# Two layers of a hybrid encoder on one core: activation tiles 2080 bytes apart, modulation blocks dealt out anew, a tenth convolution block on TensorE

## The chip, the core and the metric

The kernel runs on one core of a Trainium2 chip: TensorE (matmul), VectorE, ScalarE, GpSimd and SyncE, each with a queue of its own that it works through in order, and DMA queues between the chip's main memory and SBUF, the on-chip memory of 128 partitions. SyncE issues nearly all loads of weights. The metric is the device time of one execution, in microseconds. The time given is the median of several runs; beside it stands one profiled execution with its trace.

## The reference

An input of 256 tokens by 2048 features passes two layers, all in 32-bit floats. Each layer has a token mixer and a gated convolution feed-forward, and each of these four sub-layers f does

```
x <- x + gate * RMSNorm_post(f(RMSNorm_pre(x) * (1 + scale) + shift))
```

where shift, scale and gate (six vectors of 2048 a layer) are products of silu(c), a conditioning vector, with a matrix ada_w of 2048 by 12288 per layer. Layer 0's mixer is a convolution module: h @ w_in (2048 to 4096), a gated product, a causal depthwise convolution of width 31, a layer norm with SiLU, and @ w_out (2048 to 2048). Layer 1's mixer is gated linear attention with four heads: projections q, k, v, r and a gate, chunks of 64 tokens, @ w_out. The feed-forward is

```
a, b = split(h @ w_in)            # 2048 -> 2 * 5632
y = (silu(causal_dwconv(a, 3 taps)) * b) @ w_out
```

## The kernel before

All weights stream once through SBUF in blocks of 128 by 2048 floats, 1 MB each. The list `items` (from line 242) holds every block in the order of use. `Stream` loads them, four blocks ahead (eight during the convolution mixer), from SyncE: `load` takes a buffer from the pool `raw`, or from a second pool `cols` of four buffers for the modulation blocks that belong to layer 0's mixer and to shift and scale of its feed-forward. `_process` splits a weight block in two halves of 1024 columns: `hi`, a rounded copy made by ScalarE (line 120), and `lo`, the rest, made by VectorE (line 124). Matrix products are then sums of products of hi and lo parts. The pool `parts` holds four halves of hi and four of lo, so the split is at most one or so blocks ahead of TensorE.

The modulation vectors come from blocks of ada_w that are dealt among the weight blocks with `fill` (rows) and `fillc` (columns). A *row* block holds 128 outputs, and VectorE multiplies it with silu(c), laid out in all partitions, and sums along it, in one instruction (line 361, `ada_row`). A *column* block goes through TensorE (line 376, `ada_col`), whose result is transposed by VectorE and summed by small matmuls (line 392). A row or column block's work is done when the stream passes it (`flush`).

Two forms of product matter. `mm_block` has a weight block stationary and an activation tile moving: a matmul of 512 columns for hi (256 tokens, high and low part of the activation side by side, line 438) and one of 256 columns for lo (line 440), in runs of eight each. It serves fa and fb, the two halves of the feed-forward's first product, and q, k, r of the attention. `mm_tokens` has the activation stationary and 512 columns of weights moving (lines 609 to 611, three matmuls for a contraction tile and a token half): `ps_fo`, the second feed-forward product, `ps_cout` and `ps_gout`, the mixers' output products, and `ps_v`. The activation tiles are 128 by 512 floats, 2048 bytes in a partition, sixteen of them: the normed tiles h (and uc, the convolution's result) in `hpool`, the feed-forward's u and the attention's o in `upool`. A few weight blocks are split into hpool tiles (`st.spare`, line 974 and others), so that the last column group has all its weights at hand.

The convolution mixer (line 685) first runs the steps of h @ w_in (`ps_cin`). Then a loop (line 880) interleaves, per turn: one early column block, seven steps of the convolution on TensorE (`taps_pe`), eight taps on VectorE (`taps_dve`, line 801, 30 for a block of 128 channels), and the sums for the layer norm (`statistics`). Of sixteen channel blocks nine (`PE_BLOCKS`) go over TensorE: 16 matmuls that lay out shifted copies (`ps_late`, line 829), 32 with tap matrices `zt` built by VectorE (line 839) or ScalarE (line 843), into `ps_conv` (line 845). Seven go over VectorE. After the loop, four more column blocks fill TensorE while VectorE finishes the layer norm, and then the output product runs column group by column group. `ROWS_COUT` and `COLS_COUT` say how many modulation blocks lie behind each of its sixteen weight blocks; 16 rows (shift of the feed-forward) and 4 columns lie there.

In the feed-forward (line 944) 44 pairs of fa and fb run in groups of 16, 16 and 12; behind each group come its ps_fo blocks, four column groups of four (or three) blocks. A row block lies behind each pair from the fourth on, and behind each ps_fo block but the last three. When a gate's sixteen rows are in, GpSimd writes the gate to main memory and reads it back into all partitions (`gate_rows`, line 589).

Of the kernel before, what the change touches and what calls it, by code (L numbers as in the profile page):

```python
# [7 lines left out]
F32 = mybir.dt.float32  # L8
F32R = mybir.dt.float32r
BF16 = mybir.dt.bfloat16  # L10
AF = mybir.ActivationFunctionType
ALU = mybir.AluOpType

P = 128
D = 2048
# [9 lines left out]

RUN = 8

PE_BLOCKS = (5, 7, 9, 10, 11, 12, 13, 14, 15)

NA = 12  # L30

STEPS = ((0, 2, 0, 16), (2, 2, 0, 16), (4, 4, 0, 16), (8, 4, 0, 8), (12, 4, 0, 8), (8, 8, 8, 16))

ADA = ((2, 1, 1, 0), (3, 3, 2, 0), (1, 1, 1, 1, 1, 1, 1, 1), (3, 3, 2, 0), (1,) * 4, (1,) * 8)
COLS_CONV = 12

GLA_ORDER = [
    (w[:-1], int(w[-1]))
# [6 lines left out]
    ).split()  # L45
]
COLS_COUT = (0, 0, 0, 0), (0, 1, 0, 1), (0, 1, 0, 1), (0, 0, 0, 0)
ROWS_COUT = (0, 0, 0, 4), (2, 1, 2, 1), (2, 1, 2, 1), (0, 0, 0, 0)
GROUPS = ((0, 16), (16, 16), (32, 12))


# [12 lines left out]
class Stream:  # L64
# [3 lines left out]
    def __init__(self, tc, ctx, items, ada_row, ada_col, raw_bufs=4, split_bufs=4):  # L68
        self.tc = tc
        self.nc = tc.nc  # L70
        self.items = items
        self.ada_row = ada_row
        self.ada_col = ada_col
        self.raw = ctx.enter_context(tc.tile_pool(name="raw", bufs=raw_bufs))
        self.parts = ctx.enter_context(tc.tile_pool(name="parts", bufs=split_bufs))
        self.cols = None
        self.ahead = raw_bufs
        self.loaded = 0
        self.done = 0
        self.pos = 0  # L80
        self.raws = {}
        self.tiles = {}
        self.late = []

        self.spare = {}
        self.sums = []
        self.hold = None
        self.first = SPLIT_FIRST
        self.index = {it["key"]: i for i, it in enumerate(items)}
# [87 lines left out]
        return (lambda a, w=P: part(his, a, w)), (lambda a, w=P: part(los, a, w))  # L177


class Later(list):  # L180


# [9 lines left out]
def trunk_kernel(ctx: ExitStack, tc: tile.TileContext, x, cvec, ccol, adar, adac, adah, par, taps, wgate,  # L192
                 cin, cout, gin, gv, gout, fin, fout, out):
    nc = tc.nc
    V, A, G = nc.vector, nc.scalar, nc.gpsimd
    PS = bass.MemoryType.PSUM

    const = ctx.enter_context(tc.tile_pool(name="const", bufs=1))
    hpool = ctx.enter_context(tc.tile_pool(name="hpool", bufs=16))
    ypool = ctx.enter_context(tc.tile_pool(name="ypool", bufs=8))  # L200
    dram = ctx.enter_context(tc.tile_pool(name="dram", bufs=2, space=bass.MemoryType.DRAM))
    small = ctx.enter_context(tc.tile_pool(name="small", bufs=2))
# [5 lines left out]

    pr = const.tile([P, NPAR], F32, tag="pr", name="pr")
    A.dma_start(out=pr[:, :C_DWB], in_=par[:, :C_DWB])  # L210
    ones = const.tile([P, P], F32, tag="ones", name="ones")
    G.memset(ones, 1.0)
    zeros = const.tile([P, 1], F32R, tag="zeros", name="zeros")
    G.memset(zeros.bitcast(F32), 0.0)
    epsb = const.tile([P, 1], F32, tag="epsb", name="epsb")
    G.memset(epsb, EPS)
    onec = const.tile([P, 1], F32, tag="onec", name="onec")
    G.memset(onec, 1.0)
    table = const.tile([P, 1], F32, tag="table", name="table")
    A.activation(table, onec, AF.Silu)  # L220

# [22 lines left out]
    def item(kind, key, src, n=D):  # L244
        early = key[0] == "col" or key[:2] == ("row", 0) and key[2] != 5
        items.append(dict(kind=kind, key=key, src=src, n=n, early=early))

    def wblk(key, src, n=2048):
        item("w", key, src, n)

    rows, cols = [], []

    def fill(n):
        for l, m, k in rows[:n]:
            item("row", ("row", l, m, k), adar[l, m * KT + k])
        del rows[:n]

    def fillc(n):
        for l, m, k, nk, i in cols[:n]:
            item("col", ("col", l, m, k, nk, i), adac[m, k // 4, i] if nk == 4 else adah[1 - m, k // 2, i])  # L260
        del cols[:n]
# [31 lines left out]
                else:  # L293
                    fillc(1)
    assert not ada
    early_cols = list(cols[: COLS_CONV + 4])
    fillc(COLS_CONV + 4)
    for c in range(4):
        for i in range(4):
            wblk(("cout", c, i), cout[i, c])  # L300
            n = COLS_COUT[c][i]
            fillc(n)
            fill(ROWS_COUT[c][i])
    assert not cols
    assert not rows

    def ffn_items(l):
        for g, (p0, np_) in enumerate(GROUPS):
            for j in range(p0, p0 + np_):
                wblk(("fa", l, j), fin[l, j])  # L310
                wblk(("fb", l, j), fin[l, NF + j])
                fill(j > 2)
            for c in range(4):
                for i in range(np_ // 4):
                    wblk(("fo", l, g, c, i), fout[l, p0 // 4 + i, c])
                    fill(g < len(GROUPS) - 1 or c < 3)

    rows += [(0, 5, k) for k in range(KT)]
    rows += [(1, m, k) for k in range(KT) for m in (1, 0)]
# [79 lines left out]
    apool = {}  # L399
# [12 lines left out]
    pp = {"ps": ctx.enter_context(tc.tile_pool(name="psum", bufs=6, space=PS))}  # L412
# [45 lines left out]
        return A.activation(junk, src, AF.Square, accum_out=ss[t][:, c : c + 1])  # L458

    def new_sums(name):  # L460
        return [small.tile([P, 4], F32, tag=f"ss{t}", name=f"ss{name}{t}") for t in range(2)]

    def most(ss, name):

        b = small.tile([P, 1], F32, tag="tb", name="tb" + name)
        V.tensor_reduce(b, ss[:, :3], mybir.AxisListType.X, ALU.add)
        V.tensor_scalar(b, b, 1.0 / D, EPS, ALU.mult, ALU.add)
        return b

    def token_rstd(ss, b, name):  # L470
        r = small.tile([P, 1], F32, tag="tr", name="tr" + name)
        apool["root"] = A.activation(r, ss[:, 3:], AF.Sqrt, bias=b, scale=1.0 / D)
        V.reciprocal(r, r)
        return r

    def warm(func, src):

        d = small.tile([P, 1], F32, tag="warm", name="warm")
        A.activation(d, src[:, :1], func, scale=0.0, bias=onec)

    def rstd_of(acc, n, name):
# [17 lines left out]
    def token_diag(ss, name):  # L499

        r = token_rstd(ss, most(ss, name), name)
        dg = small.tile([P, P], F32, tag="dgx", name="dgx" + name, bufs=2)
        apool["dg"] = V.tensor_scalar_mul(dg, ident, r)
        return dg
# [180 lines left out]
    def conv_mixer(l):  # L685
        with early as cx:
# [4 lines left out]
            ss = new_sums("in")  # L691
# [82 lines left out]
            def gather(j, ps, last):  # L774
# [7 lines left out]
                if last:  # L782
# [4 lines left out]
                    V.tensor_mul(zp, zp, g)  # L787
                    if j in PE_BLOCKS:
                        on_pe.append((j, zp))
# [87 lines left out]
            apool["sums"] = lambda name: pp["ps"].tile([P, 2 * T], F32, tag="ps", name=name)  # L877
            gap = early_cols[COLS_CONV:]
            del early_cols[COLS_CONV:]
            while len(squared) < KT:  # L880
# [7 lines left out]
            assert not early_cols  # L888
            zs = [zs[j] for j in range(KT)]
            warm(AF.Sqrt, mean_a)  # L890
            r = small.tile([P, T], F32, tag="rstd", name="r_ln", bufs=1)
            line = []
# [15 lines left out]
            with tc.high_priority(SPLIT_FIRST):  # L908
# [7 lines left out]
                root = A.activation(r, r, AF.Sqrt, bias=epsb)  # L916
# [21 lines left out]
                st.spare["cout", 3, i] = st.cols, "raw", D  # L938
            dg = proj_out("cout", us, l, 1, 2, room)
            st.ahead = 4  # L940
        pp["u"] = ctx.enter_context(tc.tile_pool(name="upool", bufs=16))
        return dg

    def ffn(l, dg, last):
# [265 lines left out]
def program():  # L1210
    import concourse.bacc as _bacc

    nc = _bacc.Bacc("TRN2", target_bir_lowering=False, num_devices=1)
    args = [nc.dram_tensor(f"in_{n}", s, F32, kind="ExternalInput").ap() for n, s in _DRAM]
    args.append(nc.dram_tensor("out_0_dram", (2, P, D), F32, kind="ExternalOutput").ap())
    with tile.TileContext(nc) as tc:
        trunk_kernel(tc, *args)
    return nc


def layout(inp):
# [21 lines left out]
    late = late.transpose(1, 4, 2, 3, 0).reshape(P, KT, 32)  # L1243
    taps[:, PE_BLOCKS] = late[:, PE_BLOCKS]
    fw = g["ffn_conv_w"].reshape(2, FW, NF, P).transpose(3, 0, 2, 1).reshape(P, 2 * NF * FW)
# [30 lines left out]
```

## Time and profile before

| | |
|---|---|
| median of 3 runs | 2356.03 us (2354.91 to 2356.15) |
| profiled execution, its own time | 2360.2 us |
| its span, first to last instruction | 2358.5 us |
| mean granted clock of TensorE | 0.988 |
| TensorE busy | 2301.0 us (98%) |
| VectorE busy | 1767.7 us (75%) |
| ScalarE busy | 1208.9 us (51%) |
| read from main memory | 604.69 MB, 257 GB/s over the span |

The span is from the first to the last instruction of the profiled execution; its time holds 1.7 us around that. A matmul's duration in the trace is longer than the distance to the next one, as matmuls are pipelined: the distance of two starts is its cost in a dense run. Rows of the trace that are quoted below give start, duration (or busy time), engine, line, operation, output and inputs by the program's names, the shapes, a count (x8) and, in brackets, how long the engine had been idle and what ended that.

### The profile page before, as it was taken

To read this page: it belongs to the slowest core of one execution; us is meant where nothing else is said; L and a number is where in the kernel's file an instruction comes from. 1 tells how busy PE (TensorE), PEld (TensorE's weight loads), DVE (VectorE), ACT (ScalarE), POOL (GpSimd) and SP (SyncE) were. 2 spreads that over 40 slices of the span, in tenths; PEclk is the share of its full clock that TensorE was granted. 3 is DMA by queue.
4 is the path that set the end of the run, shared out by engine and by line. 5 is a ranking of instruction groups with operands and counts; after the bars stand their busy time and mean duration, and the time that the engine had idled before them with its cause. 6 is when DMAs were issued, how large, how long until landed. Compare 5 with 4: busy or idle time off the path is not lost.

```text
span 2358.5 us, 34325 instructions
## 1 busy us (share of the span) xinstructions
PE 2301.0 (98%) x13616; PEld 1935.1 (82%) x13616; DVE 1767.7 (75%) x2550; ACT 1208.9 (51%) x1884; POOL 16.8 (1%) x44
## 2 busy tenths in 40 slices
PE   7999998899999999999999999999999999999998
PEld 5888756688878888888888888888888888888886
DVE  3889979688878888878977877756887466655665
ACT  5334354565534554345565576656554455534553
POOL 0000000000000000000000000000000000000000
PEclk8999999899999999999999999999999999999999
DMA  9988767667799878988947756463778555555553
GB/s 385 368 325 342 286 198 300 253 236 293 288 301 355 296 286 320 362 280 314 362 161 265 277 211 229 165 229 130 294 273 282 196 188 190 196 182 195 194 202 120
DMA packets 86722, 609.05 MB, mean 258 GB/s; under 512 B 10081, under 2 KB 10401, under 8 KB 13601
## 3 DMA queue, kind: packets, MB, share of 16 engines
q1 hardware_dynamic: 84944, 602.47, 69.4%
q0 software_dynamic: 1472, 4.23, 0.7%
q8 instruction: 106, 1.74, 0.3%
q14 instruction: 56, 0.45, 0.1%
q10 hardware_dynamic: 144, 0.16, 0.0%
HBM read 604.69 MB, written 2.13 MB: 257 GB/s over the span
## 4 chain that ended last, share of the span: by engine, by line
PE 91%; DVE 4%; DMA 3%; issue 1%; ACT 1%; SPq 0%; another core or an unknown queue 0%; DVEq 0%; ACTq 0%
PE ps_fb L438 14%; PE ps_fa L438 13%; PE ps_fa L440 7%; PE ps_fb L440 7%; PE ps_fo L610 7%; PE ps_fo L611 7%; PE ps_fo L609 7%; PE ps_r L438 3%; PE ps_cin L870 2%; PE ps_cin L872 2%; PE ps_cin L871 2%; DMA raw<-in_adar 2%; PE ada L376 1%; DVE pair L801 1%; PE ps_k L438 1%; PE ps_r L440 1%
## 5 line engine op out<-in xcount | busy, mean ns | idle before, releaser
L124 DVE TENSOR_TENSOR lo<-raw,hi 128x1024 fp32r<-128x1024 f32 (+1 forms) x763 | 914.4, 1210 | 383.1 <-ACT hi L120 380.3
L120 ACT CAST hi<-raw 128x1024 fp32r<-128x1024 f32 (+1 forms) x760 | 786.1, 1044 | 809.6 <-PE ps_fa L438 183.6
L438 PE MATMUL ps_fa<-h,hi 128*128 128x512 f32 x1376 | 348.7, 395 | 0.0
L438 PE MATMUL ps_fb<-h,hi 128*128 128x512 f32 x1376 | 348.1, 395 | 0.0
L361 DVE CUSTOM_DVE_ANT_0 raw<-raw,cb 128x2048 f32<-128x2048 f32 x140 | 319.8, 2285 | 33.7 <-DMA raw<-in_adar 33.3
L438 PEld LDWEIGHTS ps_fa<-h,hi 128*128 128x128 f32 x1376 | 246.1, 188 | 46.1
L438 PEld LDWEIGHTS ps_fb<-h,hi 128*128 128x128 f32 x1376 | 245.8, 188 | 45.8
L610 PE MATMUL ps_fo<-lo,u 128*128 128x512 f32 x704 | 274.9, 390 | 5.0 <-DVE lo L124 5.0
L611 PE MATMUL ps_fo<-hi,u 128*128 128x512 f32 x704 | 274.7, 390 | 0.0
L609 PE MATMUL ps_fo<-hi,u 128*128 128x512 f32 x704 | 273.8, 390 | 0.0
L440 PEld LDWEIGHTS ps_fa<-h,lo 128*128 128x128 f32 x1376 | 182.5, 188 | 16.0 <-DVE lo L124 0.5
L440 PEld LDWEIGHTS ps_fb<-h,lo 128*128 128x128 f32 x1376 | 182.5, 188 | 15.6
L440 PE MATMUL ps_fa<-h,lo 128*128 128x256 f32 x1376 | 185.0, 277 | 0.0
L440 PE MATMUL ps_fb<-h,lo 128*128 128x256 f32 x1376 | 184.8, 277 | 0.0
L610 PEld LDWEIGHTS ps_fo<-lo,u 128*128 128x128 f32 x704 | 132.6, 188 | 32.9 <-DVE lo L124 5.4
L611 PEld LDWEIGHTS ps_fo<-hi,u 128*128 128x128 f32 x704 | 132.6, 188 | 27.7
L609 PEld LDWEIGHTS ps_fo<-hi,u 128*128 128x128 f32 x704 | 132.6, 188 | 27.6
L870 PE MATMUL ps_cin<-h,hi 128*128 128x256 f32 x512 | 146.3, 289 | 6.1 <-ACT hi L120 3.8
L872 PE MATMUL ps_cin<-h,lo 128*128 128x256 f32 x512 | 142.3, 283 | 1.6 <-DVE lo L124 1.6
L871 PE MATMUL ps_cin<-h,hi 128*128 128x256 f32 x512 | 143.6, 283 | 0.1
L870 PEld LDWEIGHTS ps_cin<-h,hi 128*128 128x128 f32 x512 | 98.6, 193 | 22.3 <-ACT hi L120 10.9
L872 PEld LDWEIGHTS ps_cin<-h,lo 128*128 128x128 f32 x512 | 98.0, 194 | 2.0 <-DVE lo L124 2.0
(265 smaller groups left out, 2754.1 us busy)
## 6 DMA issues: line engine op xcount, KB each, us to landing
raw<-in_fin SPq DMA_DIRECT2D x176, 1024.0 KB, 4.8
raw<-in_adar SPq DMA_DIRECT2D x140, 1024.0 KB, 6.4
raw<-in_fout SPq DMA_DIRECT2D x88, 1024.0 KB, 5.1
raw<-in_adac SPq DMA_DIRECT2D x44, 1024.0 KB, 6.9
raw<-in_gin SPq DMA_DIRECT2D x33, 1024.0 KB, 4.9
raw<-in_cin SPq DMA_DIRECT2D x32, 1024.0 KB, 11.4
raw<-in_cout SPq DMA_DIRECT2D x16, 1024.0 KB, 7.8
raw<-in_gv SPq DMA_DIRECT2D x16, 1024.0 KB, 4.9
```

What stands on the lines that cost most here:

```text
L120: nc.scalar.copy(hi[:, :w], r[:, s : s + w])
L124: nc.vector.tensor_sub(lo[:, o : o + n], r[:, s + o : s + o + n], hi[:, o : o + n].bitcast(F32))
L361: V.tensor_tensor_reduce(out=r, in0=r, in1=cb, scale=1.0, scalar=0.0, op0=ALU.mult, op1=ALU.add, accum_out=mod[l, m][:, k : k + 1])
L376: nc.tensor.matmul(ps[32 * (j % 4) : 32 * (j % 4) + 32], cz[:, kt], r[:, j * n : (j + 1) * n], start=kt < 4, stop=kt >= KT - 4, tile_posit ...
L438: nc.tensor.matmul(ps, hi(k * P), act[k], start=k == 0, stop=False)
L440: nc.tensor.matmul(ps[:, :T], lo(k * P), act[k][:, :T], start=False, stop=k == nk - 1)
L609: nc.tensor.matmul(pv, ah, wh, start=kt == 0, stop=False)
L610: nc.tensor.matmul(pv, ah, wl, start=False, stop=False)
L611: apool["tok"] = nc.tensor.matmul(pv, al, wh, start=False, stop=kt == nk - 1)
L870: nc.tensor.matmul(ps[:, b], hi(o), ah, start=k == 0, stop=False)
L871: nc.tensor.matmul(ps[:, b], hi(o), al, start=False, stop=False)
L872: nc.tensor.matmul(ps[:, b], lo(o), ah, start=False, stop=k == nk - 1)
```

## The change

Four things change; the computation stays the same.

First, `Spaced` wraps `hpool` and `upool`: each tile is allotted 520 floats and its first 512 are used, so that tiles lie 2080 bytes apart instead of 2048. Beside it, the 128 by 128 tile `ones` is now a broadcast of one column, the small tiles of `most` and `token_rstd` become two further columns of the sums' tile, and `warm` has one buffer instead of two. By that everything allotted behind these pools and tiles lies elsewhere too.

Second, channel block 8 is added to `PE_BLOCKS`: ten blocks over TensorE, six over VectorE.

Third, among the early column blocks 14 instead of 12 run in the convolution loop and two instead of four behind it, and seven rows are dealt among the fourteen, one behind every second column block. Of the sixteen rows of the output product nine remain.

Fourth, in the feed-forward's first group the pairs from the fourth on have one row each and a second one at every odd number and at 14, and the ps_fo blocks one behind every second instead of behind each. Groups two and three are as they were.

```diff
-PE_BLOCKS = (5, 7, 9, 10, 11, 12, 13, 14, 15)
+PE_BLOCKS = (5, 7, 8, 9, 10, 11, 12, 13, 14, 15)
...
-COLS_CONV = 12
+COLS_CONV, ROWS_CONV, COLS_NORM = 14, 7, 2
...
-ROWS_COUT = (0, 0, 0, 4), (2, 1, 2, 1), (2, 1, 2, 1), (0, 0, 0, 0)
+ROWS_COUT = (0, 0, 0, 1), (1, 1, 1, 1), (1, 1, 1, 1), (0, 0, 0, 0)
...
+class Spaced:
+    def __init__(self, pool):
+        self.pool = pool
+
+    def tile(self, shape, dtype, tag, name):
+        t = self.pool.tile([P, 512 + 8], dtype, tag=tag, name=name)[:, :512]
+        return t.rearrange("p (a b) -> p a b", b=shape[2]) if len(shape) == 3 else t
...
-    hpool = ctx.enter_context(tc.tile_pool(name="hpool", bufs=16))
+    hpool = Spaced(ctx.enter_context(tc.tile_pool(name="hpool", bufs=16)))
...
-    ones = const.tile([P, P], F32, tag="ones", name="ones")
-    G.memset(ones, 1.0)
...
+    ones = onec.to_broadcast([P, P])
...
-    early_cols = list(cols[: COLS_CONV + 4])
-    fillc(COLS_CONV + 4)
+    early_cols = list(cols[: COLS_CONV + COLS_NORM])
+    for i in range(COLS_CONV):
+        fillc(1)
+        fill(i % 2 and i // 2 < ROWS_CONV)
+    fillc(COLS_NORM)
...
                 wblk(("fb", l, j), fin[l, NF + j])
-                fill(j > 2)
+                fill((j > 2) + (g == 0 and (j % 2 and j > 2 or j == 14)))
...
                     wblk(("fo", l, g, c, i), fout[l, p0 // 4 + i, c])
-                    fill(g < len(GROUPS) - 1 or c < 3)
+                    fill(g == 1 or g == 0 and i % 2 == 0 or g == 2 and c < 3)
...
-        return [small.tile([P, 4], F32, tag=f"ss{t}", name=f"ss{name}{t}") for t in range(2)]
+        return [small.tile([P, 6], F32, tag=f"ss{t}", name=f"ss{name}{t}") for t in range(2)]
...
-        b = small.tile([P, 1], F32, tag="tb", name="tb" + name)
+        b = ss[:, 4:5]
...
-        r = small.tile([P, 1], F32, tag="tr", name="tr" + name)
-        apool["root"] = A.activation(r, ss[:, 3:], AF.Sqrt, bias=b, scale=1.0 / D)
+        r = ss[:, 5:]
+        apool["root"] = A.activation(r, ss[:, 3:4], AF.Sqrt, bias=b, scale=1.0 / D)
...
-        d = small.tile([P, 1], F32, tag="warm", name="warm")
+        d = small.tile([P, 1], F32, tag="warm", name="warm", bufs=1)
...
-        pp["u"] = ctx.enter_context(tc.tile_pool(name="upool", bufs=16))
+        pp["u"] = Spaced(ctx.enter_context(tc.tile_pool(name="upool", bufs=16)))
```

## The prediction

> **What bounds the kernel now.** I read the page's engine totals and its chain of waits first, then busy time by stretch around the convolution mixer, then the order of time inside those stretches, and last the pitch of single matmuls, start to start.
>
> ```profile
> span 2358.5 us, 34325 instructions
> PE 2301.0 (98%) x13616; PEld 1935.1 (82%) x13616; DVE 1767.7 (75%) x2550; ACT 1208.9 (51%) x1884; POOL 16.8 (1%) x44
> PE 91%; DVE 4%; DMA 3%; issue 1%; ACT 1%; SPq 0%; another core or an unknown queue 0%; DVEq 0%; ACTq 0%
> ```
>
> TensorE is the bound: 91% of the chain. So time can come from two places alone: the few stretches where TensorE waits, and the pitch of its matmuls. The waits sit here (columns: stretch, length, busy time of each engine with instructions, granted clock, DMA share, GB/s):
>
> ```profile
> 258.00:300.00 42.00, 40.36 (x622) 26.71 (x614) 41.81 (x110) 16.61 (x48) 0.00 (x0) 1.00 0.84 305
> 300.00:338.00 38.00, 35.37 (x455) 19.01 (x456) 26.75 (x60) 22.98 (x76) 3.26 (x5) 1.00 0.50 150
> 338.00:344.60 6.60, 4.89 (x61) 1.71 (x59) 6.09 (x15) 3.56 (x8) 0.23 (x1) 1.00 0.78 253
> 344.60:370.00 25.40, 25.36 (x111) 20.21 (x112) 23.48 (x51) 20.51 (x38) 0.00 (x0) 0.93 0.56 216
> 370.00:395.00 25.00, 24.73 (x112) 19.36 (x111) 25.00 (x25) 11.28 (x14) 0.00 (x0) 1.00 0.89 335
> 395.00:436.00 41.00, 27.96 (x127) 18.17 (x126) 32.79 (x37) 11.31 (x16) 0.00 (x0) 0.81 1.00 404
> 436.00:460.40 24.40, 24.40 (x97) 19.84 (x97) 12.37 (x18) 9.86 (x19) 0.00 (x0) 0.90 0.58 214
> ```
>
> From 258 to 338 runs the convolution loop, with TensorE and VectorE both full up to 300; from 344.6 to 460.4 the output projection ps_cout. In its stretch 395 to 436 the DMA is busy for its whole length, TensorE for 28 of 41 us, and the clock falls to 0.81. That is the one long place where DMA is the bound. The order of time shows the stalls in it and, later, the other one, in the first feed-forward:
>
> ```profile
> 404.11 0.40 PE L611 MATMUL ps_cout<-hi,uc 128*128 128x512 f32 x1
> 409.62 1.93 PE L376 MATMUL ada<-raw,cz 128*32 128x512 f32 x8 [5.11 <-DMA raw<-in_adac]
> 415.71 1.22 PE L609 MATMUL ps_cout<-hi,uc 128*128 128x512 f32 x2 [4.16 <-ACT hi L120]
> ...
> 656.87 15.52 DMA raw<-in_adar
> 672.52 2.29 DVE L361 CUSTOM_DVE_ANT_0 raw<-raw,cb 128x2048 f32<-128x2048 f32 x1 [10.18 <-DMA raw<-in_adar]
> 676.01 0.79 PE L610 MATMUL ps_fo<-lo,u 128*128 128x512 f32 x1 [4.97 <-DVE lo L124]
> 677.03 0.63 PE L609 MATMUL ps_fo<-hi,u 128*128 128x512 f32 x1
> 679.16 0.63 PE L611 MATMUL ps_fo<-hi,u 128*128 128x512 f32 x1
> ```
>
> A late modulation row (adar) holds VectorE, which is in order; the weight split behind the row (lo, L124) is late, and TensorE with it.
>
> **The change, part by part.**
>
> *Convolution loop.* Block 8 leaves VectorE and goes to TensorE. On VectorE the taps of line 801 go, 30 of them; on TensorE come 32 "late" matmuls and 64 of ps_conv (instructions, as f32 takes two). Six of the seven rows dealt among the fourteen columns run in the loop too, each a VectorE reduction (L361); the seventh falls behind the normalization. Two columns move from the gap after the loop into it.
>
> ```profile
> 258.00:300.00 42.00, 35.29 (x91) 1.00 0.84 305
> 310.38 1.61 PE ps_late L829 x25
> 324.25 3.35 PE ps_conv L845 x57
> 399.34 1.07 PE L376 MATMUL ada<-raw,cz 128*32 128x512 f32 x8
> 400.33 0.50 PE L610 MATMUL ps_cout<-lo,uc 128*128 128x512 f32 x1
> 606.41 2.29 DVE L361 CUSTOM_DVE_ANT_0 raw<-raw,cb 128x2048 f32<-128x2048 f32 x1
> 608.62 1.22 DVE L124 TENSOR_TENSOR lo<-raw,hi 128x1024 fp32r<-128x1024 f32 x1
> ```
>
> The first row is line 801 alone: 35.29/91 = 0.388 us a tap, so 30 taps free 11.6 us of VectorE. A row costs it 608.62 - 606.41 = 2.21 us, six cost 13.3; one more zt (0.6) makes VectorE's balance +2.3 us. TensorE gains 1.61 x 32/25 + 3.35 x 64/57 = 5.8 us, and two columns of 0.99 us (399.34 to 400.33): +7.8 us. TensorE was full up to 300 and had 2.6 us free of 38 behind it, so I take **+7 us**, near TensorE's own sum. Bounds: -4, if the loop goes by VectorE, which had 11.3 us free after 300 and is rid of the taps early (the part of the 11.6 that the rows in the full stretch don't take back); +21, if each of the six rows stands in front of a zt for which TensorE waits (7.8 + 13.3). Queued behind a row whose transfer is late are taps, then zt, then TensorE's next block.
>
> *The gap.* With two columns instead of four TensorE is busy some 2 us less of 6.6, while VectorE's normalization sets the end (6.09 of 6.60 busy). I take 0. The clock is the risk: after the 5 us wait at 670 the matmuls ran at (679.16 - 677.03)/5 = 0.43 us instead of 0.23 for about ten matmuls, 2 us; so 0 to +2.
>
> *Output projection.* Of sixteen rows nine are left beside its 16 weight blocks and 4 columns. TensorE's own work is 384 matmuls of 0.229 us (row below) and 4 columns: 92 us, of 115.8. The loss is 23.9 us. Bytes moved from 344.6 to 436: 25.4 x 216 + 25 x 335 + 41 x 404 = 30.4 MB. Seven rows are 7.3 MB, 18 us at 404 GB/s. What is left, 23 MB, takes 57 us at that rate, less than TensorE's 70 us for the first three column groups (three quarters of its work). VectorE too is relieved by 7 x 2.21 = 15 us, where it was 25.0 of 25.0 busy. I take **-17 us**, leaving 7 for starts and for VectorE; bounds -23.9 and 0 (buffers, not bytes, set the pace).
>
> *First feed-forward.* Eight rows move from the ps_fo blocks of group 0 to the fa/fb pairs. The load on DMA behind the stall falls from 2 to 1.5 MB a block of 5.44 us (24 matmuls of 0.227), 385 to 289 GB/s. The whole stall is 5.1 us plus the 2 us at half pace, 7.1. But the wait came with GpSimd's write and broadcast of the gate, which waits for the last row of (0,5); this now comes in around pair 13, in a stretch of two rows a pair: 4 MB in 11.09 us, 378 GB/s. GpSimd's wait in the stretch of the stall, and VectorE's load in four pairs:
>
> ```profile
> POOL row L595 <- DVE m L592: 317.3, 1, 317.3
> ...
> 543.49:587.86 44.37, 44.37 (x258) 38.66 (x257) 36.96 (x49) 23.47 (x37) 0.00 (x0) 1.00 0.77 284
> ```
>
> Four pairs with a row each take 36.96 us of VectorE, so a pair with two rows 36.96/4 + 2.21 = 11.4 of 11.09 us: just over full. I take **-4 us** (-7.1 and 1 for VectorE, 2 for a smaller stall at the broadcast); bounds -7.1 and +4 (eight such pairs at 0.3, and a second wait of some 2 us).
>
> *Tiles 2080 bytes apart.* This touches the pitch. Rows of the products with h moving, of ps_fo with weights from their own pool, of one ps_fo block whose weights lie in the h pool (spare, line 974), and of ps_v:
>
> ```profile
> 501.89 2.02 PE L438 MATMUL ps_fb<-h,hi 128*128 128x512 f32 x8
> 503.75 1.07 PE L440 MATMUL ps_fb<-h,lo 128*128 128x256 f32 x8
> 504.66 0.62 PE L438 MATMUL ps_fa<-h,hi 128*128 128x512 f32 x2
> ...
> 695.21 0.39 PE L611 MATMUL ps_fo<-hi,u 128*128 128x512 f32 x1
> 699.97 0.39 PE L611 MATMUL ps_fo<-hi,u 128*128 128x512 f32 x1
> ...
> 1192.80 0.39 PE L609 MATMUL ps_fo<-hi,u 128*128 128x512 f32 x1
> 1195.60 0.39 PE L609 MATMUL ps_fo<-hi,u 128*128 128x512 f32 x1
> ...
> 1261.85 0.39 PE L609 MATMUL ps_v<-hi,h 128*128 128x512 f32 x1
> 1266.66 0.39 PE L609 MATMUL ps_v<-hi,h 128*128 128x512 f32 x1
> ```
>
> ps_fo: 21 matmuls in 4.76 us, 226.7 ns. The same loop with weights in the h pool: 12 in 2.80 us, 233.3. ps_v, with h stationary: 21 in 4.81, 229.0. Eight wide and eight narrow products of fb: 2.77 us, where ps_fo's pace per column would make 2.72; so 6.7 ns over per wide one. Nothing differs but where the operands lie. I add up the pools: tiles of h start 320 bytes off the weights' offset in a cycle of 512 bytes, tiles of u at the same offset. That gives three points: moving and stationary at distance 0 cost 0, at 192 (ps_v) 2.3 ns, at 320 6.7 ns. With 2080 bytes each slot lies 32 bytes further, so sixteen slots take every distance once, u's too. At the mean of the three points, 3.0 ns, the products with h win 3.7 ns and those with u lose 3.0:
>
> ```profile
> L438 PE MATMUL ps_fa<-h,hi 128*128 128x512 f32 x1376 | 348.7, 395 | 0.0
> L438 PE MATMUL ps_r<-h,hi 128*128 128x512 f32 x256 | 65.5, 398 | 0.0
> L609 PE MATMUL ps_fo<-hi,u 128*128 128x512 f32 x704 | 273.8, 390 | 0.0
> L609 PE MATMUL ps_gout<-hi,o 128*128 128x512 f32 x128 | 49.8, 389 | 0.0
> ```
>
> Wide ones with h: 1376 twice (fa, fb), 256, and some 240 of q and k: 3248, 12.0 us won. With u: 3 x (704 + 128) = 2496, 7.5 us lost; ps_v and ps_cout 0.5. **-4 us**. Bounds: all at 226.7 wins 21.7 + 1.8 = 23.5; all u products at 233.3 lose 16.6, and the narrow ones (3248, and 1536 of ps_cin), if they paid 3.3, 15.9: +32.5, with nothing won.
>
> [...]
>
> *The rest.* ones becomes a broadcast of one column, and sums share a tile: the same instructions, 0, within 1 us either way.
>
> **The sum**: 7 - 17 - 4 - 4 = -18 us. The profiled execution took 2360.2 us (span 2358.5 and 1.7 around it), so 2342.2 on its scale; the runs' median is 2356.0, 4.2 less: **2338 us**.
>
> **Rivals.**
> - *The spacing changes no pitch.* For it: ps_fo is even over all sixteen slots; against it 233.3 beside 226.7. The others alone make -14: 2342. [...]
> - *The spacing clears the pitch everywhere*, as a distance that changes each matmul never meets twice: -14 - 23.5, 2318.5.
> - *The spacing spreads the slow pitch* (the slower side): place, every matmul that read u at distance 0; price up to 32.5 us, so 2374.5; it decides from 14 us on, when 43% of those matmuls pay in full. For it: ps_fo now has the best pace there is and can only lose.
> - *The loop eats the projection's gain*: rows in front of zt, +21, no gain in the feed-forward: 21 - 17 - 4 = 0, 2356.
>
> **How the numbers follow.** Forecast 0.40, no pitch changed 0.20, cleared 0.12, spread 0.14, eaten 0.14. A measurement can tell about 0.2%, 4.7 us. Faster: the first three and 0.02 of the last, 0.74; slower: 0.12 of "spread" and 0.02 of "eaten", 0.14; the same 0.12. The range, 2314 to 2364, takes in the cleared case and "eaten", and leaves out the upper part of "spread" and the ends of all bounds together; the forecast's own range is 2328 to 2348.
>
> **What would show it.** Convolution loop: the first ps_cout some 7 us later, ten blocks in ps_conv. Projection: no wait on in_adac or in_adar, about 99 us from the first ps_cout to the first ps_h. Feed-forward: the 4.97 us at ps_fo gone, no new ones in fa/fb from pair 3 on. Spacing: eight wide and eight narrow products in 2.72 to 2.77 us and varying, ps_fo between 226.7 and 233.3. I am wrong if ps_fo stands at 233 throughout, or if waits of VectorE on in_adar appear in the convolution loop.

## The result, and the profile after

The changed kernel takes **2381.94 us** (median of 4 runs, 2379.58 to 2383.51), the kernel before, beside it, 2356.09 us (2354.91 to 2358.23). The ratio is **1.0104, with a 95% interval of 1.0088 to 1.012**: slower by 1%, where 2338 us, 0.8% faster, was forecast. The profiled execution took 2379.58 us.

The page of the changed kernel, its span, busy time by engine and the chain of waits by engine:

```profile
span 2377.9 us, 34504 instructions
PE 2332.3 (98%) x13712; PEld 1948.2 (82%) x13712; DVE 1753.9 (74%) x2521; ACT 1215.3 (51%) x1905; POOL 16.6 (1%) x43
PE 94%; DVE 3%; DMA 2%; ACT 1%; issue 0%; SPq 0%; DVEq 0%; ACTq 0%
```

TensorE was 91% of the chain and is now 94%: waits have gone, as foreseen. But TensorE is busy for 31.3 us more than before (2332.3 against 2301.0) with 96 instructions more, which is far more than a tenth convolution block costs. The convolution loop and the output projection, by stretches (columns as in the prediction), first the kernel before:

```profile
257.92:344.64 86.72, 80.70 (x1136) 47.52 (x1129) 74.77 (x184) 43.19 (x131) 3.49 (x5) 1.00 0.69 233
344.64:460.43 115.79, 102.47 (x442) 77.59 (x443) 93.60 (x128) 52.96 (x86) 0.00 (x0) 0.90 0.79 308
```

then the changed one:

```profile
260.74:357.06 96.32, 88.37 (x1240) 49.41 (x1233) 76.40 (x166) 48.86 (x153) 3.48 (x5) 1.00 0.87 298
357.06:459.77 102.71, 99.21 (x434) 76.10 (x435) 80.22 (x116) 52.99 (x86) 0.00 (x0) 0.95 0.68 265
```

The loop grew by 9.6 us: 7.7 us of TensorE's work (88.37 - 80.70) and 1.9 us more of its waiting. The projection shrank by 13.1 us; TensorE waits there for 3.5 us, not 13.3. The two together have won 3.5 us, and at the end of the projection the changed kernel is ahead, 459.77 against 460.43.

From there on it falls behind in every stage of dense matmuls. The groups of the two kinds of product (last but one column: mean duration in ns; for ps_fo it is 390 where the starts lie 226.7 ns apart, 395 at 232.6), before, where the prediction has not shown them:

```profile
L440 PE MATMUL ps_fa<-h,lo 128*128 128x256 f32 x1376 | 185.0, 277 | 0.0
L609 PE MATMUL ps_v<-hi,h 128*128 128x512 f32 x128 | 50.1, 391 | 0.6 <-DVE k L449 0.6
```

and after:

```profile
L453 PE MATMUL ps_fa<-h,hi 128*128 128x512 f32 x1376 | 348.0, 394 | 0.0
L455 PE MATMUL ps_fa<-h,lo 128*128 128x256 f32 x1376 | 190.0, 281 | 0.1
L624 PE MATMUL ps_fo<-hi,u 128*128 128x512 f32 x704 | 277.5, 395 | 0.0
L624 PE MATMUL ps_v<-hi,h 128*128 128x512 f32 x128 | 50.7, 396 | 0.0
L624 PE MATMUL ps_gout<-hi,o 128*128 128x512 f32 x128 | 50.5, 395 | 0.0
```

The wide products with h have become 1 ns shorter (395 to 394), the narrow ones 4 ns longer (277 to 281), and the token products with u, 390 before, 5 ns longer. Two groups of ps_fo in the second layer have no wait in either kernel; with the 384 matmuls of ps_fo alone, before:

```profile
1799.02:1886.07 87.05, 87.05 (x384) 71.89 (x384) 0.00 (x0) 3.98 (x7) 1.00 0.68 215
```

after:

```profile
1810.46:1899.78 89.32, 89.32 (x384) 71.93 (x384) 0.00 (x0) 4.00 (x7) 1.00 0.52 184
```

87.05/384 is 226.7 ns a matmul, 89.32/384 is 232.6. The clock is 1.00 in both. And the runs of eight narrow and eight wide products, before:

```profile
1651.12 1.07 PE L440 MATMUL ps_fb<-h,lo 128*128 128x256 f32 x8
1652.03 2.02 PE L438 MATMUL ps_fb<-h,hi 128*128 128x512 f32 x8
1653.89 1.07 PE L440 MATMUL ps_fb<-h,lo 128*128 128x256 f32 x8
```

after:

```profile
1650.30 1.10 PE L455 MATMUL ps_fb<-h,lo 128*128 128x256 f32 x8
1651.24 2.01 PE L453 MATMUL ps_fb<-h,hi 128*128 128x512 f32 x8
1653.09 1.10 PE L455 MATMUL ps_fb<-h,lo 128*128 128x256 f32 x8
```

Eight narrow ones went from 0.91 to 0.94 us, eight wide ones from 1.86 to 1.85.

Below, the *excess* of a matmul is the distance from its start to the next one's, less 226.7 ns (512 columns, ps_fo before) or 113.3 ns (256, the narrow ones before from the second of a run on), as a mean over all dense matmuls of its kind in a trace (up to 60 ns of excess; longer ones are waits). Wide and narrow are those of fa, fb and r. Times 3000 wide and 2997 narrow products with h, 2485 token products with u and 722 of ps_v and ps_cout, the excesses of the two traces give:

| kind | excess before, ns | after, ns | difference in all, us |
|---|---|---|---|
| wide, h moving | 6.06 | 5.54 | -1.6 |
| narrow, h moving | 0.71 | 4.45 | +11.2 |
| token, u stationary | 0.29 | 5.93 | +14.0 |
| ps_v, ps_cout | 2.41 | 5.73 | +2.4 |

That is 26 us, and it covers the loss: the spans differ by 19.4 us, after what the other parts of the change have won. The table leaves out ps_cin, which is narrow too: some 1430 matmuls, 1.3 ns before and 4.5 after, 4.6 us more. The stage of ps_cin took 232.4 us before and 234.1 after; seven other kernels at the same distance modulo 256 took 228.6 to 232.0 us for it, so this loss is partly hidden in the scatter of that stage.

### The profile page after: what moved, and what is told of

It is laid out like the page before. It is cut to its first block, busy times and chain, and to the rows that moved or that the text cites. A ratio compares the mean times of both kernels' runs of the same rounds, so it can differ in the third digit from the quotient of the medians.

```text
span 2377.9 us, 34504 instructions
## 1 busy us (share of the span) xinstructions
PE 2332.3 (98%) x13712; PEld 1948.2 (82%) x13712; DVE 1753.9 (74%) x2521; ACT 1215.3 (51%) x1905; POOL 16.6 (1%) x43
## 4 chain that ended last, share of the span: by engine, by line
PE 94%; DVE 3%; DMA 2%; ACT 1%; issue 0%; SPq 0%; DVEq 0%; ACTq 0%
PE ps_fa L453 13%; PE ps_fb L453 13%; PE ps_fo L625 7%; PE ps_fo L626 7%; PE ps_fo L624 7%; PE ps_fa L455 7%; PE ps_fb L455 7%; PE ps_cin L885 3%; PE ps_cin L887 3%; PE ps_r L453 3%; PE ps_cin L886 2%; PE ada L391 1%; PE ps_cout L624 1%; PE ps_cout L625 1%; PE ps_cout L626 1%; PE ps_r L455 1%
## 5 line engine op out<-in xcount | busy, mean ns | idle before, releaser
L626 PE MATMUL ps_fo<-hi,u 128*128 128x512 f32 x704 | 277.9, 395 | 0.0
L624 PE MATMUL ps_fo<-hi,u 128*128 128x512 f32 x704 | 277.5, 395 | 0.0
L455 PE MATMUL ps_fa<-h,lo 128*128 128x256 f32 x1376 | 190.0, 281 | 0.1
L455 PE MATMUL ps_fb<-h,lo 128*128 128x256 f32 x1376 | 189.8, 281 | 0.0
L626 PEld LDWEIGHTS ps_fo<-hi,u 128*128 128x128 f32 x704 | 132.2, 188 | 31.3
L885 PEld LDWEIGHTS ps_cin<-h,hi 128*128 128x128 f32 x512 | 97.5, 191 | 22.2 <-ACT hi L122 11.6
L886 PEld LDWEIGHTS ps_cin<-h,hi 128*128 128x128 f32 x512 | 97.8, 191 | 0.9 <-DVE pair L796 0.8
```

The source lines that it names most:

```text
L455: nc.tensor.matmul(ps[:, :T], lo(k * P), act[k][:, :T], start=False, stop=k == nk - 1)
L624: nc.tensor.matmul(pv, ah, wh, start=kt == 0, stop=False)
L626: apool["tok"] = nc.tensor.matmul(pv, al, wh, start=False, stop=kt == nk - 1)
L885: nc.tensor.matmul(ps[:, b], hi(o), ah, start=k == 0, stop=False)
L886: nc.tensor.matmul(ps[:, b], hi(o), al, start=False, stop=False)
```

## The experiments

**The two halves apart.** `deal_only` has all of the change but the spacing; a tile that nothing uses, 160 bytes wide, keeps the weights as far from h as before (320 bytes modulo 512).

```diff
-hpool = Spaced(ctx.enter_context(tc.tile_pool(name="hpool", bufs=16)))
+hpool = ctx.enter_context(tc.tile_pool(name="hpool", bufs=16))
...
+small.tile([P, 40], F32, tag="pad", name="pad", bufs=1)
...
-pp["u"] = Spaced(ctx.enter_context(tc.tile_pool(name="upool", bufs=16)))
+pp["u"] = ctx.enter_context(tc.tile_pool(name="upool", bufs=16))
```

`space_only` is the reverse: the changed kernel with `PE_BLOCKS`, the early columns, `ROWS_COUT` and both `fill` lines of the feed-forward as before.

> The changed kernel with its dealing and its tenth block, but with the tiles of both pools 2048 bytes apart again and 160 bytes put in, so that h and weights lie as far apart as before (distance 320 in a cycle of 512 bytes, all tiles alike). Theory 'spacing': the spacing alone made the kernel slower; loop +9.6, output projection -13.1, first feed-forward about -4.6 as the trace after shows them, so about 2348 us, eight wide products of fb again at 2.77 us with their eight narrow ones and ps_fo at 226.7 ns. Rival 'dealing': the dealing costs time by itself, 2365 or more.

> The changed kernel with the old dealing and nine blocks: spacing of 2080 bytes and the smaller tiles alone. Theory 'spacing': the pitches of the trace after (5.9 ns over on 2491 matmuls with u, 5.5 on 3248 wide ones with h where it was 6.7, 4.5 on 3248 narrow ones, some 3 more on ps_v, ps_cout and ps_cin) add to +30 us: 2386 us, ps_cout's stall and ps_fo's wait as before. Rival 'dealing': within 10 us of 2356.

Measured beside 2360.74 us before: deal_only 2352.22 us, ratio 0.9968 (0.9956 to 0.998); space_only 2387.39, ratio 1.0116 (1.0101 to 1.0131). The dealing wins a third of a percent, the spacing loses 1.2%, and space_only shows the excesses of the changed kernel (5.53, 4.44, 5.96, 5.72 ns in the order of the table). So the whole loss comes from the 32 bytes. Part by part, the trace of deal_only has the loop at +9.8 us, the projection at -13.9, and in the first feed-forward +7.3 us in the pairs and -7.1 at ps_fo: there it wins nothing.

**Distance 0 everywhere.** ps_fo, the fastest, has moving and stationary tile at the same address modulo 512. `dist0` is the kernel before with a pad of 192 bytes, so that h too lies at distance 0 from the weights; `deal_dist0` is deal_only with 352 bytes instead of 160.

```diff
+small.tile([P, 48], F32, tag="pad", name="pad", bufs=1)
```

> The kernel before with 192 bytes put in between the h tiles and the weights, so that h, weights and u all start at the same offset in a cycle of 512 bytes; nothing else. Theory 'distance' (a steady distance of 0 between moving and stationary reads costs nothing, one of 320 costs 6.7 ns a wide matmul): fb's eight wide and eight narrow products take 2.72 us, ps_v and ps_cout go at 226.7 ns, -22 to -25 us, about 2333 us. Rival 'alignment' (only tiles that don't start at a multiple of 64 bytes pay): all lay at multiples of 64 before, so no change, 2356 us.

> The new dealing and ten blocks with tiles 2048 bytes apart and all pools at the same offset in a cycle of 512 bytes. Theory 'distance': the gains of the two add, about 2348 - 23 = 2325 us. Rival 'alignment': as with the new dealing alone, about 2348 us.

Measured: dist0 2372.20 us, ratio 1.0044 (1.0028 to 1.0061); deal_dist0 2364.58, 1.0015 (1.0005 to 1.0024). The theory that distance 0 is free held for one form only. Token matmuls obey it: 0.10 ns with u, and 0.45 for ps_v and ps_cout, which had 2.41. The wide products with h fall only to 3.4 ns, and the narrow ones, whose excess had been 0.7, rise to 5.7:

```profile
1650.35 1.12 PE L441 MATMUL ps_fb<-h,lo 128*128 128x256 f32 x8
1651.31 2.00 PE L439 MATMUL ps_fb<-h,hi 128*128 128x512 f32 x8
1653.15 1.11 PE L441 MATMUL ps_fb<-h,lo 128*128 128x256 f32 x8
```

Eight narrow ones take 0.96 us here, eight wide ones 1.84 (before 0.91 and 1.86). A price by distance exists, but wide and narrow products do not follow the same curve, and one point of a curve says nothing about the next.

**The curves.** The next kernels keep tiles 2048 bytes apart and the new dealing, and set two distances by pads: weights behind h, and u behind weights. `d192_160`, `d256_224`, `d160_0`, `w128_32` and `w32_128` are named by these two. `h2112` lets h tiles lie 2112 bytes apart, all of them at multiples of 64, and u at distance 0. As an example, d192_160 against deal_only:

```diff
-small.tile([P, 40], F32, tag="pad", name="pad", bufs=1)
+small.tile([P, 8], F32, tag="pad", name="pad", bufs=1)
...
+ctx.enter_context(tc.tile_pool(name="upad", bufs=1)).tile([P, 40], F32, tag="upad", name="upad")
 pp["u"] = ctx.enter_context(tc.tile_pool(name="upool", bufs=16))
```

> The new dealing, tiles 2048 bytes apart, weights 192 bytes beyond the h tiles and u tiles 160 beyond the weights, in a cycle of 512 bytes; all the same for every slot. Theory 'average' (each distance has a steady price, and spaced tiles pay the mean over all): wide products with h, narrow ones and the token matmuls each at a price between 0 and 9 ns, whose mean over the distances tried comes near 5.5, 4.5 and 5.9 ns. Theory 'step' (what costs is that the distance changes from one matmul to the next): most steady distances are cheap, under 3 ns for ps_fo whatever the distance.

> As the one with 192 and 160, with h to weights 256 and weights to u 224. 'Average': prices that scatter about 5.5 (wide), 4.5 (narrow) and 5.9 ns (ps_fo). 'Step': ps_fo under 3 ns.

> The new dealing, tiles 2048 bytes apart, weights and u tiles alike at 32 bytes past a multiple of 64, h tiles at a multiple of 64: distance 160 for h, 0 for u. Rival 'alignment' (an operand that doesn't start at a multiple of 64 bytes pays): ps_fo at 230 ns or more. 'Average' and 'step' alike: distance 0, so ps_fo stays at 226.7 ns; for the products with h 'step' has under 3 ns for a wide one, 'average' anything from 0 to 9.

> The new dealing, h tiles 2112 bytes apart (steps of 64 bytes, nothing off a multiple of 64), u tiles plain at distance 0. 'Alignment': products with h as cheap as with 2048 (2.77 us for eight wide and eight narrow). 'Step' and 'average': as dear as with 2080, 8 x (5.5 + 4.5) ns over 2.72, that is 2.80 us; ps_fo at 226.7 again, so some 15 us less than with both pools spaced.

> All tiles 2048 apart, weights 128 bytes past h, u 32 past the weights: the steady price of h at 128, of ps_v at 128 (the other sign) and of ps_fo at 32. Theory 'average' (2080 pays the mean of the eight steady prices, six of which are known: 0.1, 6.7, 7.6, 6.7, 2.6, 6.7 ns at 0, 64, 96, 160, 192, 224): 32 and 128 cost some 8 ns each, so that the mean is 5.8; ps_fo 234.7 ns, 90.1 us a group. Theory 'step' (with 2080 each change of distance costs by itself, whatever the distances): 32 and 128 may come out anywhere, and a mean of the eight well under 5.8 speaks for it. The whole 2365 to 2385.

> As w128_32 with the two distances exchanged: h at 32, ps_v at 224, ps_fo at 128. 'Average': ps_v 233.4 ns as ps_fo had at 224, ps_fo at 128 some 234.7 ns. 'Step': ps_fo at 128 anywhere between 226.7 and 235. Both: the same price of a token matmul at 128 here, in w128_32's ps_v and in u64's slots 8 to 11, if distance alone sets it. The whole 2365 to 2385.

One run each: d192_160 2369.36, d256_224 2380.76, d160_0 2381.17 and h2112 2373.30 us beside 2361.14 before; w128_32 2388.43 and w32_128 2391.27 beside 2361.6, both above the 2365 to 2385 that was expected. The excesses, by the address of the stationary tile less that of the moving one, modulo 256, with deal_only, dist0 and u256 (below) for the rest; a dash where no kernel had the case:

| distance | token matmul | wide, h moving | narrow, h moving |
|---|---|---|---|
| 0 | 0.1 to 0.45 | 3.4 | 5.7 |
| 32 | 6.6 | 6.3 | 5.3 |
| 64 | 6.7 | 6.1 | 0.7 |
| 96 | 7.6 | - | - |
| 128 | 5.9 | 6.0 | 5.2 |
| 160 | 6.7 | 6.5 | 6.8 |
| 192 | 2.4 to 2.9 | 2.3 | 2.5 |
| 224 | 6.7 | - | - |

The distances 32 and 128 had been expected at some 8 ns; they cost 6.6 and 5.9. The means over a run of eight also hide how a run begins. Taken one by one from the starts in the traces, the eight wide products of a run at distance 0 (dist0) cost 6.6, 9.1, 1.7, 5.7, 4.1, 0.0, 0.0 and 0.0 ns; at 64 (the kernel before) they alternate between 9.1 and 4.2 behind the first, 6.7 on average. So once a run is under way, a wide product pays what a token matmul pays at the same distance, here 0.0 and 6.7 ns (the other distances of the table agree within 0.5), and the 3.4 at distance 0 is the beginning of the run. The narrow form is the one with another curve: from the third on, each pays 6.6 to 6.7 ns at 0 and, from the second on, 0.0 at 64.

That the price repeats every 256 bytes shows in pairs: h at 0 and at 256 modulo 512 gives 3.39 and 3.44 (wide), 5.72 and 5.71 (narrow); ps_v at 256 costs 0.42, as at 0; at 128 ps_fo costs 5.87 in one kernel and ps_v 5.91 in another, and at 224 they cost 6.66 and 6.70. The theory of 64-byte alignment fell with d160_0, where u and the weights both lie 32 bytes past a multiple of 64 and ps_fo costs 0.3 ns, and with h2112, where all is aligned and the products with h cost 5.6 and 4.2 ns.

Now the price of 2080 can be read. Tiles 32 bytes further each run through all eight distances in turn. The mean of the token column is 5.4 ns (2.65 taken at 192); the changed kernel pays 5.93 and 5.73. The six known prices of the wide products have a mean of 5.1, of the narrow ones 4.4; measured 5.54 and 4.45. So **"average"** explains about nine tenths of it. It does not hold tile by tile: in the second ps_fo group of the changed kernel (from 921.69, its first three column groups, six matmuls per u tile and column group) the tiles in slots 0 and 8, at distance 0, cost 2.6 and 3.8 ns instead of 0.1, and those in slots 6 and 14, at 192, cost 6.8 and 6.7 instead of 2.4. Where the distance changes with every tile, the cheap distances lost much of their cheapness here. h2112, with four distances, pays 5.6, 4.2 and 5.1 ns where the means of the four would be 4.5, 3.5 and 3.8: there **"step"** adds 0.7 to 1.3 ns.

**Unequal distances that keep the price.** If the distance decides and not the unequal spacing, then u tiles that differ by 256 bytes must cost nothing. `u256` is deal_only with 256 bytes behind the slots 3, 7 and 11 of u; `u64` has 64 bytes there, so that four tiles each lie at 0, 64, 128 and 192.

```diff
+self.slots = []
...
-t = self.pool.tile([P, 512 + 8], dtype, tag=tag, name=name)[:, :512]
+i = len(self.slots) % 16
+self.slots.append(name)
+t = self.pool.tile([P, 512 + (64 if i in (3, 7, 11) else 0)], dtype, tag=f"{tag}{i}", name=name, bufs=1)[:, :512]
```

> Only the sixteen gated tiles u move beside deal_only: slots 0-3 and 8-11 keep distance 0 to the weights, slots 4-7 and 12-15 lie 256 bytes further. Theory 'steady price by distance, repeating every 256 bytes': at 256 the pitch is that at 0, so ps_fo stays at 226.7 to 226.9 ns, a ps_fo group of sixteen tiles at 87.05 us, the whole at deal_only's 2352. Theory 'a tile that is not at the same distance as the one before costs': 5.9 ns a matmul as with 2080, 89.3 us a group, some 2366 in all; if only the first matmuls behind each of the four changes pay, 87.1 to 87.6 us a group and 2352 to 2355.

> As u256, but with 64 bytes behind slots 3, 7 and 11: distances 0, 64, 128 and 192, each for twelve matmuls in turn. Theory 'steady price by distance': 0.1 ns at 0, 6.7 at 64 and 2.6 at 192 as other kernels show them, at 128 what the kernel with all of u there shows (some 8 by the average of the 2080 kernel): a group of sixteen +1.7 us, 88.7; the whole 2362 to 2364. Theory 'any unequal spacing costs the same': 5.9 ns at all four distances, 89.3 us, 2366.

Measured, one run each beside 2361.6: u256 2352.39 us, u64 2360.82. The same group of ps_fo as above in u256:

```profile
1791.45:1878.50 87.05, 87.05 (x384) 71.89 (x384) 0.00 (x0) 3.98 (x7) 1.00 0.54 189
```

in u64:

```profile
1795.91:1884.44 88.53, 88.52 (x384) 72.10 (x384) 0.00 (x0) 4.00 (x7) 1.00 0.54 188
```

and in w128_32, where all of u lies at 32:

```profile
1816.62:1906.21 89.59, 89.59 (x384) 71.94 (x384) 0.00 (x0) 3.97 (x7) 1.00 0.53 184
```

u256 pays nothing at all, to 0.01 us; u64 pays 3.98 ns, where the mean of the four distances is 3.8; a constant 32 costs a little more than 2080 (89.59 against 89.32 us). In u64 the price can even be read tile by tile. These are the first matmuls of the u tiles 1, 4, 7, 8, 11, 13 and 15 in one column group, six matmuls to a tile:

```profile
938.08 0.39 PE L628 MATMUL ps_fo<-hi,u 128*128 128x512 f32 x1
942.16 0.40 PE L628 MATMUL ps_fo<-hi,u 128*128 128x512 f32 x1
946.36 0.40 PE L628 MATMUL ps_fo<-hi,u 128*128 128x512 f32 x1
947.76 0.39 PE L628 MATMUL ps_fo<-hi,u 128*128 128x512 f32 x1
951.95 0.39 PE L628 MATMUL ps_fo<-hi,u 128*128 128x512 f32 x1
954.71 0.39 PE L628 MATMUL ps_fo<-hi,u 128*128 128x512 f32 x1
957.46 0.40 PE L628 MATMUL ps_fo<-hi,u 128*128 128x512 f32 x1
```

Tiles 1 to 3, at distance 0, take 4.08 us for 18 matmuls, 226.7 ns each; tiles 4 to 6, at 64, take 4.20 us, 233.3; tiles 8 to 10, at 128, take 4.19 us, 232.8; tiles 13 and 14, at 192, take 2.75 us for twelve, 229.2. Those are the prices of the constant distances, one behind the other in one kernel, and the tiles next to a border lie in between. So the distance modulo 256 sets the price wherever it stays for a few tiles, and 2080 walks through all eight, six of them dear, with too short a stay at the two cheap ones.

**The stall of the first feed-forward.** In deal_only the wait at ps_fo was gone and one of the same size stood in the pairs. Its timeline shows what comes ahead of it (start, duration, engine, instruction, and in brackets how long the engine had waited and for what):

```profile
618.10 1.17 POOL L611 DMA_DIRECT2D row<-m  x1 [271.61 <-DVE m L608]
618.97 3.77 SPq L98 DMA_DIRECT2D raw<-in_fin  x2
...
635.85 1.99 ACT L122 CAST hi<-raw 128x1024 fp32r<-128x1024 f32 x2 [9.57 <-DMA raw<-in_fin]
...
636.95 3.36 PE L454 MATMUL ps_fa<-h,hi 128*128 128x512 f32 x7 [4.82 <-ACT hi L122]
```

GpSimd writes the gate out as 2048 separate numbers. The weight block asked for 0.9 us later is there only at 635.85, 16.9 us after. What the DMA moved between 610 and 640 us, in 40 slices, and the times from issue to landing:

```profile
GB/s 404 404 350 382 404 219 153 339 415 437 350 382 404 243 253 296 131 76 33 22 44 11 121 55 33 55 44 198 340 372 295 197 22 142 208 415 448 371 470 393
...
row<-m POOLq DMA_DIRECT2D x1, 8.0 KB, 16.5
```

For 8 us the rate is 11 to 131 GB/s instead of about 400, while the DMA engines are busy for 78% of that time (622.00 to 630.25). Behind the same write of the kernel before (at 655.52 us) they are busy for 81% of 658.5 to 668 us and move 83 GB/s. `deal_trow` writes the same gate in 64 pieces of 128 bytes, behind a transpose of 32 by 32 on VectorE; `before_trow` does that alone in the kernel before; `deal_oldfill` puts the rows of the feed-forward back; `deal_oldfill_trow` does both.

```diff
-V.tensor_mul(mod[l, gate], mod[l, gate], pc(C_NG + l * 64 + which * KT, KT))
+gt, tr = (small.tile([P, 32], F32, tag=a, name=f"{a}{l}{which}", bufs=1) for a in ("gt", "gtr"))
+G.memset(gt[:, KT:], 0.0)
+V.tensor_mul(gt[:, :KT], mod[l, gate], pc(C_NG + l * 64 + which * KT, KT))
+V.transpose(out=tr, in_=gt)
...
-    G.dma_start(out=row.rearrange("k p -> p k"), in_=mod[l, gate])
+for a in range(0, P, 32):
+    G.dma_start(out=row[:, a : a + 32], in_=tr[a : a + KT])
```

> deal_only with the gate transposed on VectorE and written in 64 pieces of 128 bytes instead of 2048 numbers. Theory 'write' (the scattered write holds the DMA queues, and the weight block behind it comes late): no wait over 1 us in the first feed-forward, its first group and first ps_fo group 160.9 + 87.1 us as in the second layer, 7 us less than in deal_only; the whole 2345. Theory 'rows' (two rows a pair overload DMA and VectorE): the stall at 632 us stays, 2352. Weights lie 64 bytes past h modulo 512 instead of 320: by the price that repeats every 256 bytes the pitch does not change.

> The kernel before with the same write of the gate. Theory 'write': the stall at 670 us goes, -7 us, 2349; whether the waits on in_adac at 404 to 416 us go too is open, they come 96 us behind the write at 308 us and I expect them to stay. Theory 'rows': a row in every ps_fo block keeps the DMA full, the stall stays, 2356.

> deal_only with the feed-forward's rows dealt as before. Theory 'write': the last row of the gate comes at ps_fo again, and the write and its stall with it: 160.9 us for the first group's pairs, 94 for its ps_fo, the whole 2352 as deal_only. Theory 'rows': the stall at ps_fo comes back, the same numbers; this run tells the theories apart only together with the next.

> Rows of the feed-forward as before and the gate written in 64 pieces. Theory 'write': no stall in either place, 160.9 and 87.1 us, 2345, within 1.5 us of deal_trow. Theory 'rows': the stall at ps_fo stays at 7 us, 2352.

Measured beside 2360.3 us before:

| kernel | time, us | ratio (95%) | first group's pairs, us | its ps_fo, us |
|---|---|---|---|---|
| deal_trow | 2346.87 | 0.995 (0.9935 to 0.9965) | 160.85 | 87.06 |
| before_trow | 2348.83 | 0.9959 (0.9944 to 0.9974) | 160.85 | 87.06 |
| deal_oldfill | 2355.80 | 0.9982 (0.9973 to 0.9992) | 160.85 | 98.24 |
| deal_oldfill_trow | 2347.02 | 0.9953 (0.9936 to 0.9969) | 160.85 | 87.06 |

Theory "write" holds: with the small pieces no stall is left, wherever the rows lie. "Rows" falls: before_trow and deal_oldfill_trow have a row in every ps_fo block and lose nothing. In deal_trow the same stretch of DMA:

```profile
GB/s 459 404 437 339 448 426 142 66 360 426 426 339 393 437 376 339 307 373 200 241 415 415 382 317 426 393 317 382 393 360 208 262 470 382 251 208 240 328 393 262
...
row<-gtr POOLq DMA_DIRECT2D x4, 2.0 KB, 5.2
```

The write lands in 5.2 us, and behind it (from 618.4 us) the rate stays at 200 GB/s or more. One expectation missed: deal_oldfill has 11.2 us of stall, not 7. deal_trow beats both kernels, 0.5% under the one before. But before_trow, with the old dealing, is 0.41% under it, and the two intervals overlap: once the write is in pieces, no gain of the dealing is clear of the noise. deal_trow also has weights 64 bytes behind h modulo 512 where deal_only has 320, at the same excesses (6.06 and 0.65 ns): the period of 256 once more. The waits on in_adac stayed in before_trow, as expected.

## Why the prediction was wrong, point by point

- **The failed step is the spacing**, "Tiles 2080 bytes apart", put at -4 us; space_only measures +27 us (1.16% of 2360). The prediction's own sign of being wrong, ps_fo at 233 throughout, is what the trace shows (232.6 ns). Its finding was right: the pitch depends on the distance between moving and stationary tile. Its pricing was not. It took three points (0, 2.3 and 6.7 ns at 0, 192 and 320) for the curve, and charged their mean, 3.0 ns, to every matmul. Modulo 256 those were 0, 192 and 64, and the first two are the cheapest distances of the eight; the other five cost token matmuls 5.9 to 7.6 ns. The u products therefore paid 5.9 ns instead of 3.0, the wide ones gained 0.5 ns instead of 3.7, and the narrow ones, taken as free, rose by 3.7 ns: 11 us of the 26, and 4.6 us more in ps_cin. The narrow form had been seen at one distance only, and that is the one at which it is nearly free.
- The bounds of this step, -23.5 to +32.5, did hold the truth. The rival "spreads the slow pitch" at 2374.5 us was the case that came, 7 us short of the median. It had a chance of 0.14, and the range ended 10 us below it. With bounds this wide and no row that showed a pitch at a changing distance, the value near the middle had little behind it.
- The rival "changes no pitch", with a chance of 0.20, fell: a matmul of ps_fo takes 226.7 ns in deal_only and 233.3 in w128_32, with nothing changed but addresses. "Clears the pitch everywhere" (0.12) fell with it: at a changing distance ps_fo takes 232.6 ns. By what mechanism the addresses act, no run shows.
- **Convolution loop and gap**, +7 and 0: measured +9.6 together. TensorE's added work over loop and gap was 7.7 us, where the tenth block was to add 5.8 (the two columns only move from the gap into the loop); why it is 1.9 more, no run shows. Waits grew by another 1.9 us. The reading that TensorE and not VectorE would set the loop's length agrees with the trace: VectorE is busy for 76.40 of the 96.32 us, TensorE for 88.37, and no wait on in_adar stands there.
- **Output projection**, -17: measured -13.1, of which +1.3 is the new pitch of its 384 matmuls (3.3 ns each), so -14.4; in deal_only -13.9. The waits on in_adac went. What the step left out is a wait that has nothing to do with DMA: the column's sums wait for VectorE's transposes. Before:

```profile
434.46 0.29 PE L392 MATMUL adas<-adat,mask 128*32 128x2 f32 x8 [3.69 <-DVE adat L384]
```

after:

```profile
433.89 0.29 PE L407 MATMUL adas<-adat,mask 128*32 128x2 f32 x8 [3.50 <-DVE adat L399]
```

  It was there before. The step left 7 us of the loss for starts and VectorE without naming this wait; 9.5 stayed (23.9 - 14.4).
- **First feed-forward**, -4: the size came out, the reason did not. Apart from the pitch, the changed kernel has +0.8 us in the first pairs (162.81 against 162.00 us in the second layer) and 2.5 us of stall left at ps_fo, where there had been 7.1: -3.8 us. But the step laid the stall on the bytes of the rows. It is GpSimd's scattered write, which cost 3.3 us here, 7.1 before, 7.3 in deal_only and 11.2 in deal_oldfill; why it differs, no run shows. For the three others a kernel with the pieces shows it; for the 3.3 us of the changed kernel it is argued from the order of time alone (the write starts at 622.61 us, the late blocks follow). The write stood in the prediction as what the wait "came with"; the row of its DMA's landing time, in the kernel before, was not read:

```profile
row<-m POOLq DMA_DIRECT2D x4, 8.0 KB, 15.8
```

- *The rest* at 0: the layers' three other norm stages moved by 0.2 us at most.
- The sum without the spacing was -14; deal_only has -7.5 (0.9968 of 2360.7, interval -10 to -5), less by the projection's 3, the loop's 3 and the feed-forward's 4, with 3 us the other way in the first stage (229.6 instead of 232.4 us), which scatters by 4 us between kernels at the same distance.

## What to carry to other kernels

Where a matmul's pitch differs between two places of a kernel, compare the addresses of its moving and stationary tiles modulo 256 before anything else (here 0.1 to 7.6 ns of a token matmul hung on them), and measure the whole curve for each width of matmul; the spacing that makes the distance walk got about the mean of the curve or a little more (5.9 ns with u, where the mean is 5.4), which is worse than a good constant (0.1 ns at 0). A constant is set with a pad that nothing uses. A transfer in single numbers is judged by what lands behind it: look for a rate that collapses on busy DMA engines (83 GB/s at 81% busy, in the kernel before), and write longer pieces (here 64 of 128 bytes, which landed in 5.2 us instead of 16.5).

## What the runs showed of the hardware

- The start-to-start time of an fp32r matmul of 512 columns was 226.7 to 234.3 ns on average in these kernels, that of 256 columns 114 to 120 ns, by the distance of the two operands' addresses in SBUF, with a period of 256 bytes (3.39 and 3.44 ns of excess for the wide ones, 5.72 and 5.71 for the narrow ones, at 0 and at 256 modulo 512). At 64 the narrow ones are nearly free (0.7 ns) and those of 512 columns dear (6.1 to 6.7); at 0 the narrow ones pay 5.7 and those of 512 columns 0.0 to 0.45, but for the first five of a run of eight behind narrow ones (1.7 to 9.1). Why was not found. With a distance that changes at every tile, the cheap distances were not cheap (2.6 and 3.8 ns at 0, 6.7 and 6.8 at 192, with u in the changed kernel).
- In deal_only a write of 2048 single numbers, 8 KB, took 16.5 us to land (17.0 before, 13.4 in the changed kernel) and held up the loads issued behind it on another queue: 11 to 131 GB/s for 8 us. In 64 pieces of 128 bytes (deal_trow) it landed in 5.2 us and held up nothing that TensorE waited for (160.85 and 87.06 us for the first group). It was worth 0.4% of this kernel (before_trow, 0.9959), about as much as the whole dealing (0.9968).
